# A hybrid decoder step on one core: the first token tile is normed by a diagonal matmul, and side work in the projection phase changes engine and place

## The chip, the core and the metric

The kernel runs on one core of a Trainium2 chip. The core has five engines with queues of their own: TensorE (PE, with the weight load shown apart as PEld), VectorE (DVE), ScalarE (ACT), GpSimd (POOL) and SyncE (SP), which here only starts DMA transfers. Each engine takes its instructions in the order in which the program lists them, so an instruction that waits holds up everything behind it on its engine. The metric is the device time of one execution in microseconds (us).

## The reference

The program is one inference step of one layer with three branches. Its beginning is what the change touches. The tokens x (1024 of a prompt, 64 of a sample) are normed, multiplied by a weight matrix, and the result is cut into the inputs of the branches:

```python
def rms_norm(x, g):
    xf = x.astype(jnp.float32)
    y = xf * lax.rsqrt(jnp.mean(xf * xf, axis=-1, keepdims=True) + EPS) * g.astype(jnp.float32)
    return y.astype(x.dtype)
...
    z = rms_norm(x, gain) @ w_in
    split_at = np.cumsum(IN_SIZES)[:-1].tolist()
    (rq, rk, rv, rg, pu, pg, nq, ck, cv, sk, sv, wk, wv, nbg, ng, mg) = jnp.split(z, split_at, axis=-1)
```

Retention takes rq, rk and rv, pooling takes pu, and sparse attention takes nq and the six key and value parts ck to wv. Gates merge the three, and one more matrix gives the output. All of this is in float32, and the kernel keeps that precision by holding each number as a float16 high half and a float16 low half (the remainder). A product is then three matmuls: high by high, low by high, high by low.

## The kernel before

The 1088 tokens are nine tiles of 128 (the ninth, number 8, is the sample and has 64). The function `phase_kv` is the first phase. It fills `self.xh` and `self.xl`, the normed tokens turned so that the 1024 channels lie on the partitions in 8 slices, and it projects each tile twice: `kv_tile` makes the keys, values and branch gates (792 columns, in PSUM tiles of 512 and 280), `q_tile` makes the queries (512 columns). The loop over `n` runs over the tiles in the order `TILES` = 0 to 6, 8, 7. At step n it norms the tile two places ahead, makes the keys and values of tile n, and makes the queries of tile n-1. Each PSUM tile of 512 columns is 24 matmuls (8 slices times 3).

`norm_tile` squares a tile on ACT with a sum over the channels (L352, L355), takes the power -1/2 on POOL (`rsqrt`, L381), and multiplies x by that factor and by the norm weights `gain` on DVE (L358). Tiles 0 to 2 are then turned by PE transposes (L370) into PSUM, and ACT and DVE copy the two halves out (L373, L374). Tiles 3 and later are split first, on ACT (L361) and POOL (L362), and turned by DMA transposes (L364).

`load_t` brings the weights in 8 slices by DMA and `wsplit` splits each into halves on ACT (L218) and DVE (L219). The buffers `raw` are two; four more slices use the memory of the query weights as `spare`. `input_sums` makes eight groups of sums of the normed tokens for a later phase (four additions on POOL, L1163; four subtractions on DVE, L1165; halves on ACT and DVE, L1166 and L1167; one DMA). `load_c` brings a block of 128 columns of weights for the phase after (`self.wng`). `cmp_prompt` needs the block means `cm` that PE makes of each tile's keys and values (L591).

The order of instructions on an engine is not the order of the code. A scheduler places each instruction as early as it thinks its inputs allow, so that work written late can stand early in a queue. Two means hold it back: `issue_after(ins)` puts instructions behind `ins` on its engine, and `behind()` does that for every instruction in the dictionary `self.marks`, one for each engine. Both only order a queue; they add no wait on the chip.

The rest of the program (attention of the prompt, retention, pooling, attention of the sample, output) follows `phase_kv`, and its code is the same in both kernels. Its first matmuls are those of `silu_c` (L298 to L300), which use the block of weights `self.wng`.

Of the kernel before, what the change touches and what calls it, by code (L numbers as in the profile page):

```python
# [20 lines left out]
P = 128  # L21
# [106 lines left out]
class Kern:  # L128
# [32 lines left out]
    def run(self):  # L161
# [3 lines left out]
        with ExitStack() as es:  # L165
# [7 lines left out]
            with ExitStack() as e1:  # L173
# [7 lines left out]
                deque(self.silu_c(sp, self.gc, C_NG, ps, self.wng), 0)  # L181
# [34 lines left out]
    def wsplit(self, hi, lo, raw):  # L216
        nc = self.nc
        nc.scalar.activation(hi, raw, AF.Copy, scale=WS)  # L218
        nc.vector.scalar_tensor_tensor(lo, raw, WS, hi, op0=ALU.mult, op1=ALU.subtract)  # L219
# [15 lines left out]
    def load_t(self, pool, cols, tag, bufs, out=None, spare=(), between=None):  # L235
# [5 lines left out]
        for k in range(8):  # L241
            if between and k == 4:
                between()
            if 3 <= k < 3 + len(spare):
                raw = spare[k - 3]
            else:
                raw = self.wtile([P, 1024], F32, "raw")
# [4 lines left out]
            self.wsplit(hi[:, k, :], lo[:, k, :], raw[:, :n])  # L252
# [15 lines left out]
    def proj_t(self, out, hi, lo, t, c0, n):  # L268
# [5 lines left out]
        for k in range(8):  # L274
# [4 lines left out]
            nc.tensor.matmul(out, xl, hi[:, k, c0:c0 + n], start=False, stop=(k == 7))  # L279
# [22 lines left out]
    def evac(self, out, c0, ps, n, m):  # L302

        nc = self.nc
        if m == P:
            nc.scalar.activation(out[:, c0:c0 + n], ps[:, :n], AF.Copy, scale=IWS)
            return
# [25 lines left out]
    def norm_tile(self, xp, ps, gain, t):  # L333
        nc, d = self.nc, self.d
        m = self.tm(t)
        x = xp.tile([P, 1024], F32, tag="x", name=self.nm("x"), bufs=2)
        src = d["x_sample"].rearrange("b t c -> (b t) c") if t == 8 else d["x_prompt"][0, t * P:(t + 1) * P, :]
        if t == 0:
            nc.sync.dma_start(x[:, :512], src[:, :512])
            nc.sync.dma_start(x[:, 512:], src[:, 512:])  # L340
            nc.sync.dma_start(gain, d["norm_gain"].broadcast_to([P, 1024]))
            nc.sync.dma_start(self.ident, d["c_ident"])
            nc.sync.dma_start(self.a4, d["c_a4"])
            nc.vector.tensor_copy(self.id16, self.ident)
        else:
            nc.sync.dma_start(x[:m], src)
        xs = xp.tile([P, 1024], F32, tag="xs", name=self.nm("xs"), bufs=2)
        ss = xp.tile([P, 2], F32, tag="ss", name=self.nm("ss"), bufs=2)
        cuts = (slice(0, 512), slice(512, 1024)) if t == 0 else (slice(0, 1024),)
        if t == 0:  # L350
            for i, c in enumerate(cuts):
                nc.scalar.activation(xs[:, c], x[:, c], AF.Square, accum_out=ss[:, i:i + 1])  # L352
            nc.vector.tensor_tensor(ss[:, 0:1], ss[:, 0:1], ss[:, 1:2], op=ALU.add)
        else:
            nc.scalar.activation(xs[:m], x[:m], AF.Square, accum_out=ss[:m, 0:1])  # L355
        self.rsqrt(ss[:m, 1:2], ss[:m, 0:1], 1.0 / 1024)
        for c in cuts:
            nc.vector.scalar_tensor_tensor(xs[:m, c], x[:m, c], ss[:m, 1:2], gain[:m, c], op0=ALU.mult, op1=ALU.mult)  # L358
# [54 lines left out]
    def bias_tables(self, bp, ps):  # L413
# [19 lines left out]
        nc.vector.tensor_copy(self.idb, self.ident)  # L433
# [1325 lines left out]
```

## Time and profile before

| what | value |
|---|---|
| runs | 1335.08, 1335.47 and 1340.86 us, median 1335.47 |
| the profiled execution | 1337.31 us, span from first to last instruction 1335.5 us |
| PE busy | 1263.3 us (95% of the span) |
| DVE, ACT, POOL busy | 860.3, 613.3 and 539.4 us (64%, 46%, 40%) |
| mean granted clock of TensorE | 0.989 of full speed |

An engine's busy time says how much of the span it had an instruction in work. PE is near its limit over the whole program, so that time can only be won where PE is idle or runs at its lower clock. The page's view in 40 slices shows PE's busy tenths 6, 7, 9, 9, 9 in the first five slices of 33.4 us each, and 9 in nearly all that follow.

### The profile page before, as it was taken

Reading aid. Unit: us, or ns where it says so; the run is one execution under the profiler, and the core shown is the slowest. Engines: PE = TensorE matmul, PEld = TensorE weight load, DVE = VectorE, ACT = ScalarE, POOL = GpSimd, SP = SyncE. Lnnn points to the kernel's source line nnn. Section 1 sums busy time; section 2 is a strip of 40 time slices with the busy share of each in tenths; the row PEclk is TensorE's granted clock in tenths of the full one; section 3 lists DMA queues with packets and bytes.
Section 4 is the critical chain, followed back from the end, with each engine's and each line's share of the span. In section 5 each row is a group of like instructions: output and inputs, shape, how many; then the busy total and the mean of one; then the engine's idle time right before and its main releaser. Section 6 shows DMA issues by size and latency. Waiting matters only on the chain. (4 is left out here: it accounts for less than half of the span.)

```text
span 1335.5 us, 27663 instructions
## 1 busy us (share of the span) xinstructions
PE 1263.3 (95%) x10572; PEld 852.2 (64%) x10572; DVE 860.3 (64%) x2164; ACT 613.3 (46%) x1434; POOL 539.4 (40%) x587
## 2 busy tenths in 40 slices
PE   6799999989999998999999999999999999998997
PEld 3345566667666665555555566667888888877444
DVE  6676225777776763767684757762388777789523
ACT  6533234666666763546554443433334333333112
POOL 2346112556666662245554461101134665455100
PEclk9899999999999999999999999999999999999999
DMA  8957412577998998342554154314232211343332
GB/s 269 207 124 166 76 48 68 110 126 141 148 181 173 172 185 184 95 124 70 160 134 96 47 147 110 80 41 166 55 104 68 60 48 49 97 128 94 129 99 80
DMA packets 311210, 155.63 MB, mean 117 GB/s; under 512 B 202849, under 2 KB 297025, under 8 KB 310660
## 3 DMA queue, kind: packets, MB, share of 16 engines
q1 hardware_dynamic: 280004, 122.88, 40.9%
q10 hardware_dynamic: 26336, 17.67, 4.7%
q0 software_dynamic: 4736, 13.31, 3.2%
q8 instruction: 83, 1.36, 0.5%
q14 instruction: 51, 0.42, 0.1%
HBM read 84.91 MB, written 23.55 MB: 81 GB/s over the span
## 5 line engine op out<-in xcount | busy, mean ns | idle before, releaser
L704 POOL TENSOR_TENSOR hl<-S,hl 128x640 f16<-128x640 f32 (+7 forms) x128 | 152.2, 1198 | 157.9 <-DVE hl L703 97.3
L298 PE MATMUL pj<-xh,whi 128*128 128x384 f16 (+1 forms) x480 | 153.5, 320 | 1.7 <-ACT qsts L643 1.7
L299 PE MATMUL pj<-xl,whi 128*128 128x384 f16 (+1 forms) x480 | 153.4, 320 | 0.0
L300 PE MATMUL pj<-xh,wlo 128*128 128x384 f16 (+1 forms) x480 | 153.4, 320 | 0.0
L277 PE MATMUL z<-rwh,xh 128*128 128x512 f16 x256 | 97.0, 379 | 0.0
L279 PE MATMUL z<-rwh,xl 128*128 128x512 f16 x256 | 97.0, 379 | 0.0
L278 PE MATMUL z<-rwl,xh 128*128 128x512 f16 x256 | 97.0, 379 | 0.0
L699 ACT ACTIVATE S<-S,nm 128x640 f32<-128x640 f32 (+7 forms) x128 | 93.7, 732 | 5.1 <-DVE hl L703 1.3
L300 PEld LDWEIGHTS <-wlo 128*128 128x128 f16 x672 | 66.0, 98 | 35.5 <-issue 1.7
L1434 POOL TENSOR_TENSOR ws<-raw 128x512 f32<-128x512 f32 x12 | 15.7, 1312 | 180.4 <-DMA raw<-w_in 154.2
L218 ACT ACTIVATE whi<-raw 128x1024 f16<-128x1024 f32 (+1 forms) x53 | 48.6, 917 | 86.8 <-PE pj L299 20.6
L299 PEld LDWEIGHTS <-whi 128*128 128x128 f16 x672 | 66.0, 98 | 34.6 <-issue 3.8
L298 PEld LDWEIGHTS <-whi 128*128 128x128 f16 x672 | 66.0, 98 | 33.6 <-issue 1.4
L1698 PE MATMUL py<-wo,mm 128*128 128x512 f16 (+2 forms) x408 | 83.5, 367 | 1.0 <-ACT mm L1651 1.0
L1487 DVE TENSOR_TENSOR q<-st,q 128x288 f32<-128x288 f32 (+1 forms) x168 | 71.1, 434 | 20.0 <-PE st L1478 18.6
L1270 PE MATMUL o<-vst,pt 128*128 128x64 f16 x528 | 57.9, 194 | 22.0 <-DMA pt<-hl 22.0
L279 PEld LDWEIGHTS <-xl 128*128 128x128 f16 x448 | 44.4, 99 | 48.3 <-issue 3.9
L277 PEld LDWEIGHTS <-xh 128*128 128x128 f16 x448 | 45.2, 101 | 45.4 <-issue 5.9
L278 PEld LDWEIGHTS <-xh 128*128 128x128 f16 x448 | 44.4, 99 | 42.4 <-issue 1.8
L795 DVE CUSTOM_DVE_ANT_0 S<-pn,tnear 128x256 f32<-128x256 f32 (+1 forms) x128 | 47.2, 403 | 32.3 <-PE pn L789 27.8
L1698 PEld LDWEIGHTS <-mm 128*128 128x128 f16 x408 | 39.4, 98 | 44.6 <-ACT mm L1651 1.5
L1270 PEld LDWEIGHTS <-pt 128*128 128x128 f16 x528 | 47.5, 98 | 31.5 <-DMA pt<-hl 28.2
(469 smaller groups left out, 4002.6 us busy)
## 6 DMA issues: line engine op xcount, KB each, us to landing
raw<-w_in SPq DMA_DIRECT2D x26, 512.0 KB
raw<-w_in ACTq DMA_DIRECT2D x18, 512.0 KB
x<-x_prompt SPq DMA_DIRECT2D x14, 512.0 KB
raw<-w_in SPq DMA_DIRECT2D x48, 128.0 KB
txd<-rso SPq DMA_DIRECT2D x8, 544.0 KB
q<-egd SPq DMA_DIRECT2D x16, 272.0 KB
s<-state_ret SPq DMA_DIRECT2D x16, 256.0 KB
o_ret_s<-s POOLq DMA_DIRECT2D x16, 256.0 KB
```

What stands on the lines that cost most here:

```text
L218: nc.scalar.activation(hi, raw, AF.Copy, scale=WS)
L277: nc.tensor.matmul(out, xh, hi[:, k, c0:c0 + n], start=(k == 0), stop=False)
L278: nc.tensor.matmul(out, xh, lo[:, k, c0:c0 + n], start=False, stop=False)
L279: nc.tensor.matmul(out, xl, hi[:, k, c0:c0 + n], start=False, stop=(k == 7))
L298: nc.tensor.matmul(out, hi[:, k, :], xh, start=(k == 0), stop=False)
L299: nc.tensor.matmul(out, hi[:, k, :], xl, start=False, stop=False)
L300: nc.tensor.matmul(out, lo[:, k, :], xh, start=False, stop=(k == 7))
L699: nc.scalar.activation(s[:, c0:c1], s[:, c0:c1], AF.Exp, bias=nm[:, br:br + 1], scale=0.125, accum_out=l[:, 0, br, r:r + 1])
L704: nc.gpsimd.tensor_tensor(hl[:, w:2 * w], s[:, d0:c1], hl[:, :w], op=ALU.subtract)
L1270: nc.tensor.matmul(out, lhs[0], rhs[0], start=start, stop=False)
L1487: nc.vector.tensor_tensor(out[:, c0:c0 + n], b, x[:, c0:c0 + n], op=ALU.add)
L1698: nc.tensor.matmul(py[:, :n], mm[:, k, t, a, e:e + P], b[:, k, cq], **fl)
```

## The change

The first tile gets a function of its own, `norm_first`. The squares of its second half are summed on DVE beside those of the first half on ACT. The power -1/2 of each token is put on the diagonal of a matrix `dg` (identity times a column), and x is turned and scaled at once by an fp32 matmul of x with `dg`. The norm weights then lie along the partitions (`gcol`, 8 columns), and the copies out of PSUM multiply by them, one copy for each of the 8 slices on ACT and on DVE. The weights come as two inputs that the host lays out: `gain_cols` (128x8) and `gain_rows` (128x1024, for the other tiles, loaded later). The identity is loaded third, and `c_a4` after the weights.

The slices of the key and value weights go to the spare memory from the second on (before: from the third). The second tile's norm, the later weight splits, the sums of `input_sums`, the load of `self.wng`, and two casts are tied behind marks; `input_sums` is spread over steps 4 to 8 as 1, 2, 2, 2, 1. POOL's subtraction of `norm_tile` (L362) and its additions of `input_sums` (L1163) go to DVE. The block means of a tile (`cmp_means`) are tied behind the last projection matmul, so that they follow the query projection, and `cmp_prompt` comes after the last `q_tile`. The sample's query tile gets a buffer of its own (`qs8`).

```diff
+                with self.behind():
+                    deque(self.silu_c(sp, self.gc, C_NG, ps, self.wng), 0)
...
         for k in range(8):
-            if between and k == 4:
-                between()
-            if 3 <= k < 3 + len(spare):
-                raw = spare[k - 3]
+            if between:
+                between(k)
+            if 2 <= k < 2 + len(spare):
+                raw = spare[k - 2]
...
+            if between and k:
+                self.marks = self.first[0 if k == 1 else 1]
+            with self.behind() if between and k else nullcontext():
+                split = self.wsplit(hi[:, k, :], lo[:, k, :], raw[:, :n])
+            if between:
+                self.marks = split
...
+    def norm_first(self, xp, ps):
+
+        nc, d = self.nc, self.d
+        x = self.load_x(xp, 0)
+        nc.sync.dma_start(self.ident, d["c_ident"])
+        gcol = xp.tile([P, 8], F32, name="gcol", bufs=1)
+        nc.sync.dma_start(gcol, d["gain_cols"])
...
+        nc.scalar.activation(xs[:, :512], x[:, :512], AF.Square, accum_out=ss[:, 0:1])
+        nc.vector.tensor_tensor_reduce(out=xs[:, 512:], in0=x[:, 512:], in1=x[:, 512:], scale=1.0, scalar=0.0,
+                                       op0=ALU.mult, op1=ALU.add, accum_out=ss[:, 1:2])
+        nc.vector.tensor_tensor(ss[:, 0:1], ss[:, 0:1], ss[:, 1:2], op=ALU.add)
+        self.rsqrt(ss[:, 1:2], ss[:, 0:1], 1.0 / 1024)
+        dg = xp.tile([P, P], F32, name="dg", bufs=1)
+        nc.vector.tensor_scalar(dg, self.ident, ss[:, 1:2], None, op0=ALU.mult)
+        self.first = []
+        for q in range(2):
+            tp = ps.tile([P, 4, P], F32, tag="tk", name=self.nm("tp"), bufs=2)
+            for k in range(4):
+                kk = q * 4 + k
+                nc.tensor.matmul(tp[:, k, :], x[:, kk * P:(kk + 1) * P], dg, start=True, stop=True)
+            for k in range(4):
+                kk = q * 4 + k
+                self.marks["ACT"] = nc.scalar.activation(self.xh[:, kk, :P], tp[:, k], AF.Copy, scale=gcol[:, kk:kk + 1])
+                self.marks["DVE"] = nc.vector.scalar_tensor_tensor(
+                    self.xl[:, kk, :P], tp[:, k], gcol[:, kk:kk + 1], self.xh[:, kk, :P],
+                    op0=ALU.mult, op1=ALU.subtract)
+            self.first.append(dict(self.marks))
...
-            nc.gpsimd.tensor_tensor(xd[:m, 1], xs[:m], xd[:m, 0], op=ALU.subtract)
+            nc.vector.tensor_tensor(xd[:m, 1], xs[:m], xd[:m, 0], op=ALU.subtract)
...
-                self.kv_tile(kp, bp, ps, kh, kl, cmt, TILES[n])
+                kvz = self.kv_tile(kp, bp, ps, kh, kl, TILES[n])
+            if n:
+                self.q_tile(kp, ps, qh, ql, TILES[n - 1])
             if n == NT:
                 self.cmp_prompt(kp, ps, cmt)
-            if n:
-                self.q_tile(kp, ps, qh, ql, TILES[n - 1])
+            if n < NT and TILES[n] < 8:
+                with self.tc.issue_after(self.marks["PE"].ins):
+                    self.cmp_means(ps, kvz, cmt, TILES[n])
...
-            if n >= 5:
-                next(sums, None)
-                next(sums, None)
+            with self.behind():
+                for _ in range((0, 0, 0, 0, 1, 2, 2, 2, 1, 0)[n]):
+                    next(sums)
             if n == 7:
-                self.wng = self.load_c(d["w_in"][0][:, C_NG:C_NG + P])
+                with self.behind():
+                    self.wng = self.load_c(d["w_in"][0][:, C_NG:C_NG + P])
...
-                    nc.gpsimd.tensor_tensor(f[:, i], self.xh[:, kk, c], self.xl[:, kk, c], op=ALU.add)
+                    nc.vector.tensor_tensor(f[:, i], self.xh[:, kk, c], self.xl[:, kk, c], op=ALU.add)
```

The order of instructions differs up to about row 1550 of PE's 20519, row 184 of DVE and row 137 of ACT, and is the same from there to the end. Three places show how.

The first is the start of DVE's queue. In these rows a row is a line of code, the operation, what it writes and what it reads; `ss` is the sum and the factor of a token, `kvl` the low half of a weight slice. Before:

```order
L353 TENSOR_TENSOR ss_123<-ss_123 128x1
L380 TENSOR_SCALAR ss_123<-ss_123 128x1
L344 CAST id_67<-ident 128x128
L358 SCALAR_TENSOR_TENSOR xs_122<-x_115,ss_123,gain 128x512 x2
L433 CAST idb<-ident 128x128
L219 SCALAR_TENSOR_TENSOR kvl_148<-raw_149,kvh_147 128x792
L374 TENSOR_TENSOR xl<-tp_131,xh 128x4x128
```

And now:

```order
L362 ISA xs_121,ss_122<-x_115 128x512
L362 ISA ss_122 128x1
L364 TENSOR_TENSOR ss_122<-ss_122 128x1
L413 TENSOR_SCALAR ss_122<-ss_122 128x1
L367 TENSOR_SCALAR dg<-ident,ss_122 128x128
L220 SCALAR_TENSOR_TENSOR kvl_159<-raw_160,kvh_158 128x792
L377 SCALAR_TENSOR_TENSOR xl<-tp_130,gcol,xh 128x128 x3
```

The scaling of 2 times 512 columns by `gain` and two casts of the identity have left the place ahead of PE's first work, and one multiplication of 128 columns stands there.

The second is ACT's queue where the queries of the first tile are copied out of PSUM (`qs<-pj`). `whi<-raw` splits weights of the next phase, `xd<-xs` is a tile's high half ahead of its DMA transposes. Before:

```order
L355 ACTIVATE xs_883,ss_884<-x_881 64x1024
L228 DMA raw_1648<-w_in 128x8x128
L218 ACTIVATE whi_1388<-raw_1386 128x1024
L361 CAST xd_772<-xs_766 128x1024
L619 ACTIVATE qs_470<-pj_445 128x8x64
L218 ACTIVATE whi_1650<-raw_1648 128x1024
```

And now:

```order
L394 CAST xd_621<-xs_615 128x1024
L314 ACTIVATE kvz_510<-pj_511 128x512
L389 ACTIVATE xs_911,ss_912<-x_909 64x1024
L602 CAST kd_565<-kvz_510 128x2x128
L621 CAST vst<-kvz_510 128x2x64
L670 ACTIVATE qs_479<-pj_454 128x8x64
L394 CAST xd_786<-xs_780 128x1024
```

The split of the next phase's weights has gone from ahead of the copy (it now stands some 50 rows further down), and so has one of the halves `xd`.

The third is PE's queue at the block means `cm` of one tile, beside the query projection `pj<-nqh` or `nql` of the tile before. Before:

```order
L278 LDWEIGHTS xh
L278 MATMUL pj_686<-nql,xh 128x512
L591 MATMUL cm_681<-a_68,kvz_612 128x4 x2
L279 LDWEIGHTS xl
L279 MATMUL pj_686<-nqh,xl 128x512
```

And now:

```order
L287 LDWEIGHTS xl
L287 MATMUL pj_695<-nqh,xl 128x512
L657 MATMUL cm_724<-a_68,kvz_626 128x4 x2
L458 MATMUL btp<-oh_734,rb 32x512
```

The means stood after 8 of the 24 matmuls of the query projection, and now stand after all of them.

## Rows read from the trace of the kernel before

**Rows 1.** Busy time by stretch: start:end, us, PE, PEld, DVE, ACT, POOL (instructions), PEclk, DMA, GB/s

```profile
8.94:37.07 28.13, 23.51 (x136) 14.08 (x137) 22.93 (x37) 22.16 (x40) 9.73 (x11) 1.00 0.87 277
37.07:68.43 31.36, 23.12 (x123) 12.15 (x121) 20.29 (x35) 15.24 (x28) 11.98 (x13) 0.89 0.89 196
68.43:161.21 92.78, 86.88 (x586) 48.25 (x585) 55.24 (x110) 31.03 (x74) 40.05 (x62) 0.98 0.58 126
```

**Rows 2.** PE's waits up to 175 us: line, waited for, total us, times, longest

```profile
PE tp L370 <- DVE xs L358: 10.7, 2, 8.9
PE tq L634 <- DVE qs L620: 5.9, 1, 5.9
PE cm L591 <- ACT kvz L306: 3.2, 2, 2.7
...
PE pj L278 <- DVE nql L219: 1.2, 1, 1.2
```

**Rows 3.** Timeline of the start: start, length, engine, line, operation [idle before, releaser]

```profile
4.46 0.63 ACT L352 ACTIVATE xs<-x 128x512 f32<-128x512 f32 x1
...
5.65 0.55 POOL L381 TENSOR_TENSOR ss<-ss,half 128x1 f32<-128x1 f32 x1 [5.21 <-DVE ss L380]
...
8.00 0.23 DVE L344 CAST id<-ident 128x128 f16<-128x128 f32 x1 [2.43 <-DMA ident<-c_ident]
8.14 1.41 DVE L358 SCALAR_TENSOR_TENSOR xs<-x,ss,gain 128x512 f32<-128x512 f32 x2
...
8.94 1.97 PE L370 MATMUL tp<-ident,xs 128*128 128x128 f32 x8 [8.94 <-DVE xs L358]
...
10.73 0.84 PE L277 MATMUL pj<-kvh,xh 128*128 128x512 f16 x2
```

**Rows 4.** Two stretches of the start, columns as in Rows 1

```profile
4.46:7.60 3.14, 0.00 (x0) 0.00 (x0) 0.31 (x2) 0.73 (x4) 0.55 (x1) 1.00 0.82 266
8.00:13.00 5.00, 4.06 (x15) 2.57 (x16) 4.77 (x9) 3.77 (x6) 0.00 (x0) 1.00 1.04 409
```

**Rows 5.** Timeline, an fp32 matmul that is no transpose (four in the program)

```profile
86.75 1.06 PE L425 MATMUL btp<-oh,rb 33*32 33x512 f32 x8
```

**Rows 6.** Timeline around the first query tile

```profile
54.71 1.06 ACT L218 ACTIVATE whi<-raw 128x1024 f16<-128x1024 f32 x1 [6.16 <-DMA raw<-w_in]
...
57.65 1.05 ACT L361 CAST xd<-xs 128x1024 f16<-128x1024 f32 x1 [1.88 <-DMA xl<-xd]
...
59.97 1.03 PE L634 MATMUL tq<-id,qs 128*128 128x128 f16 x8 [5.86 <-DVE qs L620]
```

**Rows 7.** Busy time of the stretch from 58.00, columns as in Rows 1

```profile
58.00:64.80 6.80, 4.83 (x21) 2.91 (x22) 4.71 (x8) 5.59 (x10) 3.77 (x4) 0.50 0.91 202
```

**Rows 8.** Timeline at the block means of the fifth step

```profile
79.41 1.10 ACT L1166 CAST rso<-rsf 128x1088 f16<-128x1088 f32 x1 [4.47 <-DVE rsf L1165]
...
81.06 0.61 PE L591 MATMUL cm<-a,kvz 128*128 128x4 f32 x4 [2.70 <-ACT kvz L306]
...
82.00 0.63 PE L278 MATMUL pj<-nql,xh 128*128 128x512 f16 x1
...
85.58 0.38 PE L278 MATMUL pj<-nql,xh 128*128 128x512 f16 x1
```

**Rows 9.** Groups by line and shape, 0 to 161 us: busy us, mean ns, idle before

```profile
L1163 POOL TENSOR_TENSOR rsf<-xh,xl 128x272 f32<-128x272 f16 x32 | 22.3, 727 | 16.5 <-DVE rso L1167 13.1 <-DMA xl<-xd 2.2 <-DVE xl L374 1.2
...
L1165 DVE TENSOR_TENSOR rsf<-rsf 128x272 f32<-128x272 f32 x32 | 22.5, 704 | 11.6 <-POOL rsf L1163 9.7
...
L1167 DVE TENSOR_TENSOR rso<-rsf,rso 128x1088 f16<-128x1088 f32 x8 | 10.5, 1311 | 7.6 <-ACT rso L1166 7.6
```

**Rows 10.** All instructions of line 1165: ns min/median/max, first and last start us

```profile
L1165 DVE TENSOR_TENSOR rsf<-rsf x32: 371/443/2247, 66.2 to 128.8; 128x272 f32<-128x272 f32 x32
```

**Rows 11.** Timeline of the phase's end

```profile
159.10 0.43 PE L641 MATMUL tq<-id,qs 64*64 64x64 f16 x8 [0.90 <-DVE qs L628]
...
161.21 0.48 PE L298 MATMUL pj<-xh,whi 128*128 128x384 f16 x1 [1.67 <-ACT qsts L643]
```

More of the change, by code (lines that the diff above doesn't have):

```diff
@@ L278, in proj_t @@
             nc.tensor.matmul(out, xh, lo[:, k, c0:c0 + n], start=False, stop=False)
-            nc.tensor.matmul(out, xl, hi[:, k, c0:c0 + n], start=False, stop=(k == 7))
+            self.marks["PE"] = nc.tensor.matmul(out, xl, hi[:, k, c0:c0 + n], start=False, stop=(k == 7))
     def cols2(self, out, xh, xl, hi, lo, c0, n):
@@ L305, in evac @@
         if m == P:
-            nc.scalar.activation(out[:, c0:c0 + n], ps[:, :n], AF.Copy, scale=IWS)
+            self.marks["ACT"] = nc.scalar.activation(out[:, c0:c0 + n], ps[:, :n], AF.Copy, scale=IWS)
             return
@@ L470, in phase_kv, with between @@
         gain = kp.tile([P, 1024], F32, name="gain", bufs=1)
-        self.norm_tile(kp, ps, gain, 0)
+        self.norm_first(kp, ps)
+        def between(k):
+            if k == 3:
+                x = self.load_x(kp, 1)
+                nc.sync.dma_start(gain, d["gain_rows"])
+                with self.behind():
+                    self.norm_tile(kp, ps, gain, 1, x)
         nq = [wk.tile([P, 8, 512], F16, name="nq" + x) for x in "hl"]
         spare = [x.rearrange("p k c -> p (k c)").bitcast(F32)[:, o:o + 1024] for x in nq for o in (0, 1024)]
-        kh, kl = self.load_t(wk, [(C_KV, 792)], "kv", 1, spare=spare, between=lambda: self.norm_tile(kp, ps, gain, 1))
+        kh, kl = self.load_t(wk, [(C_KV, 792)], "kv", 1, spare=spare, between=between)
         cmt = kp.tile([P, 2, 32], F32, name="cmt", bufs=1)
+        nc.sync.dma_start(self.a4, d["c_a4"])
+        with self.behind():
+            nc.vector.tensor_copy(self.id16, self.ident)
         for n in range(NT + 1):
@@ L557, in kv_tile @@
         if tk is None:
-            nc.sync.dma_start_transpose(self.kst[:, :, rows], kd.rearrange("p r g b a c -> p (r g b a c)"))
+            self.marks["SP"] = nc.sync.dma_start_transpose(self.kst[:, :, rows], kd.rearrange("p r g b a c -> p (r g b a c)"))
         elif t < 8:
@@ L587, in kv_tile @@
         if t < 8:
-            nc.vector.reciprocal(self.gate[:, t, :], ge)
-            cmps = ps.tile([P, 2, 4], F32, tag="cm", name=self.nm("cm"))
-            for a in range(2):
-                nc.tensor.matmul(cmps[:, a, :], kvz[:, a * P:(a + 1) * P], self.a4, start=True, stop=True)
-            for a in range(2):
-                nc.vector.tensor_scalar(cmt[:, a, 4 * t:4 * t + 4], cmps[:, a, :], self.pm[:, a:a + 1], None,
-                                        op0=ALU.add)
+            self.marks["DVE"] = nc.vector.reciprocal(self.gate[:, t, :], ge)
         else:
@@ L608, in kv_tile, with cmp_means @@
                                         ap=[[1, 8], [24, 8], [1, 1]]))
+        return kvz
+    def cmp_means(self, ps, kvz, cmt, t):
+        nc = self.nc
+        cmps = ps.tile([P, 2, 4], F32, tag="cm", name=self.nm("cm"))
+        for a in range(2):
+            nc.tensor.matmul(cmps[:, a, :], kvz[:, a * P:(a + 1) * P], self.a4, start=True, stop=True)
+        for a in range(2):
+            nc.vector.tensor_scalar(cmt[:, a, 4 * t:4 * t + 4], cmps[:, a, :], self.pm[:, a:a + 1], None, op0=ALU.add)
     def q_tile(self, kp, ps, qh, ql, t):
@@ L626, in q_tile @@
             nc.scalar.copy(qs[:64], qz[:, :, None, :].to_broadcast([64, 8, 2, 64]))
-            qt = kp.tile([P, 8, 2, 64], F16, tag="qs", name=self.nm("qs"))
+            qt = kp.tile([P, 8, 2, 64], F16, tag="qs8", name=self.nm("qs"), bufs=1)
             nc.vector.tensor_tensor(qt[:64, :, 0, :], qz, qs[:64, :, 0, :], op=ALU.subtract)
```

45 lines of the change are left out of this document (22 added, 23 removed).

## The prediction

> **What bounds the kernel now.** I read the busy shares first: PE is busy for 95% of the span, so only the places where it idles or runs slowly can pay. The view by stretch shows where these are. The change reorders the queues only up to the first matmul of `silu_c`, at 161.21 us, so I cut the time before it. PE does nothing for 8.94 us; then it is busy for 23.51 of 28.13 us, for 23.12 of 31.36 us at a mean clock of 0.89, and for 86.88 of 92.78 us at 0.98 [rows 1]. So the first 68 us hold most of what can be won.
>
> The list of PE's waits names the causes. The longest are the first transposes waiting for the scaled x, 8.9 us, then one wait of 5.9 us of the first query tile's transposes for `qs`, and 3.2 us in which the block means wait for a copy on ACT [rows 2]. The timelines then show what was late in each case.
>
> At the start, POOL has the factor of each token ready at 5.65 + 0.55 = 6.20 us. DVE, however, stands at the cast of the identity until its DMA lands at 8.00 (2.43 us idle), then scales 2 times 512 columns, and PE starts at 8.94 [rows 3]. The identity's transfer is queued behind the broadcast of the norm weights. In this time the DMA engines move 266 GB/s, against 409 GB/s a little later when the weight slices come [rows 4].
>
> At 59.97 PE has waited 5.86 us for `qs`. ACT's copy stood behind the split of `self.wng`, which had idled ACT for 6.16 us waiting for its weights, and behind a half `xd`, which had waited another 1.88 us for a DMA transpose to free its buffer [rows 6]. PE's clock then is 0.50 from 58.00 to 64.80 [rows 7].
>
> At 81.06 the block means wait 2.70 us for ACT, which had itself idled 4.47 us for the subtractions of `input_sums`; after that a 128x512 matmul takes 0.63 us instead of 0.38 [rows 8].
>
> **The change part by part.**
>
> *The start.* Removed from PE's path are the wait for the identity behind the norm weights and the scaling of 2 times 512 columns. The squares of the second half move to DVE. No row shows this reduction; the nearest is the scaling, 1.41 / 2 = 0.7 us for 512 columns, about the 0.63 us of ACT, so the sum of squares comes at most a few tenths earlier or later, and I take POOL's end at 6.2 as it is. Then one multiplication of 128 columns, for which the cast of the identity gives 0.23 us: PE starts at about 6.5 instead of 8.94. The identity now lies behind x alone, whose second half ACT read at 4.46, so I expect it by then or soon after.
>
> Against this, the eight transposes become eight plain fp32 matmuls. The fp32 matmul of `btp` shows what these cost: four in the program are eight instructions on PE, two passes each, and the four run side by side in 1.06 us, so one pass of 512 columns takes about 0.5 us at full clock and one of 128 about 0.13, or 0.26 at half clock [rows 5]. The transposes took 1.97 / 8 = 0.25 us each at the low clock [rows 3], so a pass costs what a transpose did, and there are 16. They take 3.9 us and end near 10.4; the first projection begins there instead of at 10.73. The Trainium skill ("TensorE: Matmul & The Clock Gate", section "Terms") calls the transpose mode four times faster for FP32. By that the eight matmuls would take 8 x 4 x 0.25 = 7.9 us; by the rows it is two times, and I go by the rows. The eight small copies on ACT and on DVE, at 0.23 us or so each (the cast again), lie beside these passes except the last.
>
> What PE then waits for is the stream of weight slices. The 3.14 us up to 7.60 carried 266 GB/s; at 409 GB/s the same bytes take 2.04, so the stream is 1.1 us earlier if the laid-out norm weights move like the rest. Two small transfers fewer stand ahead of the slices, some 0.5 us of issue. I take **-1.6** for this stretch. The bounds are 0 and -4.6: the first if the waits inside move, since the small matmul `pmps` now stands in PE's queue before the third slice is done and needs two transfers (`c_a4`, `pe_cmp`) that lie behind six weight slices; the second is all the idle time there, 28.13 - 23.51.
>
> *37 to 68 us.* The split of `self.wng` and one `xd` no longer stand ahead of the copy of `qs`, and the 512 KB load of that block no longer competes with the DMA transposes. Gone are 5.9 us of waiting and half of the 4.83 us that PE was busy at the low clock, 2.4 us: **-8.3**. Something comes back. In DVE's new order the low halves of the second tile's keys, for which PE waits early in the first query tile, stand behind POOL's old subtraction (1024 columns, 1.3 us by the row of 1088 columns [rows 9]), two copies of a third tile (0.7 each, by the scaling) and the scaling of the fifth tile (1.4): 4.1 us of work. PE has some other matmuls by then; I take 3.3 us of waiting, where the old order had 31.36 - 23.12 - 5.86 = 2.4 of other idle time, so +1.0. A wait of this length was followed by about 3.4 us of half clock in the old trace, which cost 1.7 [rows 8]; I add that: **+2.7** in all, between 0 and +6.8 (all 4.1 waited for, 1.7, and 1.0 more for the last query weights, whose loads now follow DMA transposes in SP's queue).
>
> *68 to 161 us.* The means go behind the query projection, by when their input is long copied, and POOL no longer delays `input_sums`: the 3.2 us of waits go, and with them the low clock of this stretch, (1 - 0.98) x 92.78 = 1.9: **-5.1**. DVE takes 32 additions of 272 columns, 0.727 us each on POOL, and POOL's six subtractions. On DVE I take 0.443, the median of the subtractions of the same size [rows 10]: 14.2 us, and 6 x 1.3 = 7.8. But the 32 subtractions had taken 22.5 us in total, up to 2.25 each, while POOL was adding; at the median they take 14.2, which gives 8.3 back. DVE's 55.24 us become at most 55.2 + 14.2 + 7.8 - 8.3 = 68.9 of some 87.7, 79%, so this is hidden. It costs when a wait of ACT or PE falls in behind a block of eight such operations, 3.5 us; the key halves and query copies have at least the 5 us of the next projection for it.
>
> *The end.* The wait of 0.90 for the buffer of the sample's queries goes with `qs8`. The wait of 1.67 for the copy `qsts` [rows 11] stays in another shape: the second pair of `cmp_prompt` matmuls now stands directly ahead of `silu_c`, and needs the small copies of the first pair, which ACT and DVE interleave with the query copies and the last `input_sums`. I reckon **+0.4**, between -2.6 (both waits gone) and +2.
>
> The sum is -1.6 - 8.3 + 2.7 - 5.1 + 0.4 = **-11.9 us**. From there on both programs have the same order and wait for the same things, so I carry it to the end. Against the profiled execution's 1337.3 us that is 1325.4; the median of the runs lies 1.8 us below that execution, so I forecast 1323.6.
>
> **The rivals.** *The waits move.* The start gives nothing because PE stands at `pmps`, and 37 to 68 us give back 6.8 instead of 2.7: -8.3 + 6.8 - 5.1 + 0.4 = -6.2, about 1329.3; a little more waiting for the query weights makes it 1332. For it speaks that ACT, DVE and SP wait in turn for each other in this stretch; against it, that the old wait had two long transfers behind it that are now elsewhere.
>
> *Plain fp32 matmuls cost four transposes each.* The first projection starts 4 us later than I reckoned and everything behind it too: 1327.6. The skill's rule above gives this; the `btp` row speaks against it.
>
> *DVE becomes the bound.* If an addition on DVE takes as long as the subtractions did at worst, DVE's work exceeds the 87.7 us that PE needs in tiles 3 to 8. That begins at 0.443 + (87.7 - 68.9) / 32 = 1.03 us each; at 1.8 it is 25 us too much, 13 more than is won, and the time is 1348. The subtractions at 2.25 us speak for it; that POOL does nothing long beside DVE any more speaks against it.
>
> *No net change.* The marks only order queues. If the scheduler's old order was waiting for the same transfers that any order must wait for, the phase ends where it did: 1335. The 6.16 us of ACT waiting for weights that nobody needed yet speaks against it.
>
> **How the numbers follow.** My forecast has a chance of 0.60, the moving waits 0.20, the dear fp32 matmuls 0.05, no change 0.07, DVE as the bound 0.08. About 0.5% (6.7 us, so below 1328.8) is what a measurement of this kernel can tell from no change. Faster by more than that are the forecast, the fp32 case and a third of the moving waits: 0.72. Within it lie the rest of the moving waits and no change, 0.20, and a weak form of the DVE case, 0.01; slower is the rest, 0.07. The range goes from 1317 (start at its bound of -4.6, nothing given back in 37 to 68 us, nothing lost at the end: -18.0 or 1317.5) up to 1333, which takes in the moving waits; outside it are most of the no-change case and DVE as the bound.
>
> **What would show it.** PE's first matmul at 6.5 us with 16 fp32 instructions at 0.25 us; the first query projection some 2 us before 37.07; no wait of PE over 3 us between 30 and 70 us, and the key projection of tile 3 begun by 60 instead of 68.43; no wait for the means; DVE's additions at 0.4 to 0.5 us; the first `silu_c` matmul at about 149 us; the same length from there to the end. I would be wrong if ACT again stood behind a transfer in front of `qs`, if PE lost its clock in the new waits more than once, or if the later phases gave the time back.

## The result and the profile after

The changed kernel takes 1323.44 us (median; 1322.17 to 1326.12) against 1338.16 us for the kernel before in the same comparison: a ratio of 0.9892, 95% interval 0.9855 to 0.9928. A second comparison on another chip gave 1323.26 us and 0.9906 (0.9882 to 0.9930). The profiled execution took 1326.12 us, with a span of 1324.4.

I cut the new trace at the same five events as the old one: the first matmul, the first query projection, the key projection of the fourth tile, the last query projection, and the first matmul of `silu_c`. Columns as in [rows 1]; first the kernel after, then the stretches of before that were not shown yet.

```profile
6.48:37.38 30.90, 27.40 (x145) 17.83 (x146) 22.56 (x45) 20.81 (x41) 3.90 (x5) 0.89 0.84 258
...
37.38:60.62 23.24, 20.81 (x123) 11.17 (x121) 14.73 (x29) 12.50 (x26) 5.64 (x8) 1.00 0.77 172
60.62:137.36 76.74, 76.74 (x536) 44.34 (x536) 49.58 (x121) 29.09 (x65) 17.81 (x33) 1.00 0.65 135
137.36:149.33 11.97, 8.14 (x50) 4.55 (x50) 10.74 (x30) 6.38 (x14) 0.00 (x0) 0.83 0.68 170
...
149.33:1324.40 1175.07, 1130.61 (x9733) 777.72 (x9732) 763.17 (x1977) 545.06 (x1291) 477.97 (x498) 0.99 0.47 111
```

```profile
68.43:151.92 83.49, 80.15 (x542) 44.93 (x540) 52.35 (x100) 26.65 (x61) 40.05 (x62) 0.98 0.61 133
151.92:161.21 9.29, 6.73 (x46) 3.33 (x46) 2.88 (x10) 4.38 (x14) 0.00 (x0) 0.96 0.34 58
161.21:1335.50 1174.29, 1129.77 (x9732) 777.68 (x9731) 759.66 (x1974) 542.27 (x1288) 476.88 (x498) 0.99 0.47 109
```

Event by event: the first query projection starts at 37.38 instead of 37.07 (+0.31); from there to the fourth key projection 23.24 instead of 31.36 [rows 1] (-8.12); to the last query projection 76.74 instead of 83.49 (-6.75), with PE busy all the time; to `silu_c` 11.97 instead of 9.29 (+2.68). The sum is -11.88, and what follows is 0.78 longer. The start gained nothing, and the end lost; the middle won more than either. The two traces thus differ by 11.1 us, the medians by 14.7 here and by 13.3 in the second comparison; the runs of the kernel before alone spread from 1335.08 to 1341.84 us in the first.

PE's waits up to 165 us, columns as in [rows 2], without the 6.5 us for its first matmul. The waits of 5.9 for `qs` and 3.2 for the means are gone; the longest between 30 and 70 us is the 1.0 for `kvz`.

```profile
PE tq L692 <- DVE qs L679: 2.0, 1, 2.0
PE vc L562 <- DVE kcst L560: 1.5, 1, 1.5
PE pj L285 <- ACT kvh L219: 1.4, 1, 1.4
PE pj L285 <- ACT kvz L314: 1.0, 1, 1.0
...
PE tk L609 <- DVE xl L407: 0.7, 1, 0.7
PE tk L609 <- ACT kd L602: 0.6, 1, 0.6
```

The timeline of the start, columns as in [rows 3], and a stretch of it, columns as in [rows 1], show why 2.5 us less before the first matmul came to nothing.

```profile
6.48 3.79 PE L373 MATMUL tp<-dg,x 128*128 128x128 f32 x16 [6.48 <-DVE dg L367]
...
8.59 0.37 ACT L376 ACTIVATE xh<-tp,gcol 128x128 f16<-128x128 f32 x1 [0.29 <-PE tp L373]
9.23 0.34 DVE L377 SCALAR_TENSOR_TENSOR xl<-tp,gcol,xh 128x128 f16<-128x128 f32 x1
...
9.61 0.37 ACT L376 ACTIVATE xh<-tp,gcol 128x128 f16<-128x128 f32 x1 [0.65 <-DVE xl L377]
...
10.01 0.35 DVE L377 SCALAR_TENSOR_TENSOR xl<-tp,gcol,xh 128x128 f16<-128x128 f32 x1 [0.43 <-ACT xh L376]
...
14.67 0.85 ACT L219 ACTIVATE kvh<-nqh 128x792 f16<-128x792 f32 x1
14.81 0.35 DVE L377 SCALAR_TENSOR_TENSOR xl<-tp,gcol,xh 128x128 f16<-128x128 f32 x1 [0.44 <-ACT xh L376]
...
15.58 0.81 PE L285 MATMUL pj<-kvh,xh 128*128 128x512 f16 x2 [1.37 <-ACT kvh L219]
...
17.17 0.77 PE L487 MATMUL pmps<-a,pe 32*128 32x1 f32 x3 [0.78 <-DMA pe<-pe_cmp]
```

```profile
15.60:22.40 6.80, 6.02 (x22) 3.91 (x22) 5.31 (x8) 5.93 (x10) 0.56 (x1) 0.50 0.65 191
```

The sixteen fp32 instructions take 3.79 us, as reckoned. But the copies take turns: the high copy of 9.61 starts when the low copy of the slice before ends (9.23 + 0.34), and the low copy of 10.01 when that high copy has ended (9.61 + 0.37). Eight pairs run from 8.59 to 15.16 us. Weight splits on ACT and DVE stand among and behind them (the low copy of 9.23 stood behind one on DVE), PE idles 1.37 us for one on ACT (14.67), and 0.78 more in `pmps`.

The larger loss follows: from 15.6 to 22.4 us the granted clock is 0.50 (1.2 GHz), where the kernel before had 1.00 [rows 1]. PE is busy for 6.02 us of it; half of that, an estimated 3.0 us, is what the clock costs. PE's idle time up to the first query projection is even less than before, 30.90 - 27.40 = 3.5 against 4.6 us; its busy time is 3.9 us more.

The Trainium skill ("PSUM — Partial Sum Buffer", section "PSUM bank collisions raise a hardware error") says that two engines must not be in one PSUM bank and partition group together, and that the compiler's scheduler puts a dependency between such accesses. The timeline agrees: the copies of the start form two sequences, as for two PSUM tiles, and within neither do two overlap.

The end, DVE and PE:

```profile
142.36 1.50 DVE L1214 TENSOR_TENSOR rsf<-xh,xl 128x272 f32<-128x272 f16 x4
...
143.77 1.22 DVE L220 SCALAR_TENSOR_TENSOR wlo<-raw,whi 128x1024 f16<-128x1024 f32 x1
144.91 0.43 DVE L1216 TENSOR_TENSOR rsf<-rsf 128x272 f32<-128x272 f32 x1
145.26 0.68 DVE L679 TENSOR_TENSOR qs<-qz,qs 64x512 f16<-64x512 f32 x1
...
145.99 0.63 PE L692 MATMUL tq<-id,qs 64*64 64x64 f16 x8 [1.98 <-DVE qs L679]
...
148.71 0.69 PE L562 MATMUL vc<-wcvd,cmr 64*128 64x64 f32 x2 [1.53 <-DVE kcst L560]
```

The last group of `input_sums` and a weight split stand in DVE's queue ahead of the sample's queries, which PE waits 1.98 us for.

### The profile page after: what moved, and what is told of

Its sections match the earlier page's. It is cut to its first block, busy times and chain, and to the rows that moved or that the text cites. A ratio compares the mean times of both kernels' runs of the same rounds, so it can differ in the third digit from the quotient of the medians.

```text
span 1324.4 us, 27672 instructions
## 1 busy us (share of the span) xinstructions
PE 1263.7 (95%) x10580; PEld 855.6 (65%) x10580; DVE 863.0 (65%) x2209; ACT 615.9 (47%) x1438; POOL 506.1 (38%) x549
```

## The experiments

My theory after the result: the gain is the wait of ACT's queue for `self.wng`, the means in the middle of a projection, and POOL's slow work; the start is eaten by the copies' turns; the end is lost to the late sums. The rivals are in the expectations. One table holds the events of all traces (start in us of the first query projection, the fourth key projection, the last query projection and `silu_c`; the rest of the span behind that; then the median of the runs, and its ratio to the kernel before in the same comparison, with the 95% interval).

| kernel | query 1 | key 4 | last query | silu_c | rest | median | ratio |
|---|---|---|---|---|---|---|---|
| before | 37.07 | 68.43 | 151.92 | 161.21 | 1174.3 | 1338.16 | 1 |
| changed | 37.38 | 60.62 | 137.36 | 149.33 | 1175.1 | 1323.44 | 0.9892 (0.9855 to 0.9928) |
| e_again (changed) | 36.80 | 58.88 | 135.62 | 147.58 | 1173.8 | 1323.26 | 0.9906 (0.9882 to 0.9930) |
| e_wng | 37.52 | 62.42 | 142.16 | 155.56 | 1175.9 | 1331.92 | 0.9964 (0.9935 to 0.9993) |
| e_pool | 37.87 | 60.66 | 141.40 | 151.76 | 1176.2 | 1329.57 | 0.9946 (0.9923 to 0.9970) |
| e_cmmid | 36.23 | 57.57 | 138.75 | 151.10 | 1172.6 | 1325.80 | 0.9922 (0.9895 to 0.9948) |
| e_oldstart | 36.25 | 55.90 | 133.45 | 145.47 | 1176.7 | 1325.84 | 0.9912 (0.9885 to 0.9938) |
| e_oldstart2 (the same) | 38.77 | 58.44 | 135.99 | 148.26 | 1176.0 | 1322.03 | 0.9895 (0.9871 to 0.9920) |
| e_copies | 35.51 | 55.96 | 134.15 | 146.09 | 1177.8 | 1323.27 | 0.9886 (0.9835 to 0.9937) |
| e_sums | 36.77 | 59.19 | 135.94 | 146.33 | 1172.9 | 1323.23 | 0.9899 (0.9868 to 0.9929) |
| e_all | 35.11 | 54.77 | 132.32 | 142.74 | 1172.9 | 1322.50 | 0.9897 (0.9871 to 0.9923) |
| e_all2 (the same) | 32.32 | 52.91 | 133.92 | 144.40 | 1180.2 | 1323.05 | 0.9902 (0.9872 to 0.9933) |
| e_oldall | 38.79 | 58.44 | 135.99 | 146.97 | 1179.8 | 1326.30 | 0.9915 (0.9887 to 0.9943) |
| e_best | 35.33 | 54.99 | 133.58 | 143.60 | 1178.3 | 1320.49 | 0.9879 (0.9850 to 0.9908) |

The same code differs from trace to trace by up to 2.8 us in an event of the front and by 7.3 us in the rest (e_all, e_all2), so single traces tell only larger things apart.

**The load let loose (e_wng).**

```diff
-                with self.behind():
-                    deque(self.silu_c(sp, self.gc, C_NG, ps, self.wng), 0)
+                deque(self.silu_c(sp, self.gc, C_NG, ps, self.wng), 0)
...
             if n == 7:
-                with self.behind():
+                if True:
                     self.wng = self.load_c(d["w_in"][0][:, C_NG:C_NG + P])
```

> Only the load of the output gates' weights and its split are let loose again (not tied behind marks), all else as changed. Theory: the 8.1 us gained between the first query projection and the fourth key projection are the wait of ScalarE's queue for this load; so that stretch goes back from 23.2 us to 29 to 32 us, ScalarE shows a wait of 4 us or more before the split, and the time is 1329 to 1332 us. Rival: the gain comes from the other edits of this stretch (the low halves on VectorE, the order of the copies); then the stretch stays at 23 to 25.5 us, the split waits under 2 us, and the time is 1323 to 1326 us.

ACT's timeline has the wait back, in two pieces:

```profile
54.75 1.06 ACT L218 ACTIVATE whi<-raw 128x1024 f16<-128x1024 f32 x1 [2.70 <-DMA raw<-w_in]
...
60.53 1.06 ACT L218 ACTIVATE whi<-raw 128x1024 f16<-128x1024 f32 x1 [3.19 <-DMA raw<-w_in]
...
61.50 0.58 ACT L669 ACTIVATE qs<-pj 128x512 f16<-128x512 f32 x1
61.97 0.40 ACT L313 ACTIVATE kvz<-pj 128x280 f32<-128x280 f32 x1
```

Behind the second split stand the copies of `qs` and `kvz`; PE waits 3.6 us for the latter, up to 62.42, and from 60.6 us on its granted clock is 0.50:

```profile
37.52:62.42 24.90, 20.36 (x115) 10.71 (x113) 15.75 (x29) 13.60 (x27) 5.55 (x8) 0.96 0.92 206
60.60:67.40 6.80, 4.91 (x18) 2.08 (x18) 4.71 (x9) 4.96 (x10) 0.55 (x1) 0.50 0.85 199
62.42:142.16 79.74, 79.67 (x545) 45.56 (x545) 53.32 (x131) 30.22 (x67) 17.59 (x33) 0.97 0.65 138
142.16:155.56 13.40, 7.66 (x50) 4.18 (x50) 7.60 (x21) 5.06 (x13) 0.00 (x0) 0.89 0.61 140
```

The mechanism and the median (8.5 us over the changed kernel) are the theory's. The size in its stretch is not: 24.90 instead of 29 to 32, which lies in the rival's range of 23 to 25.5. Beside 1.8 us for the wait (62.42 - 60.62), the next stretch is 3.0 longer (79.74 - 76.74; by its mean clock of 0.97 about 2.4 of that is the low clock) and the end loses 1.4. So this edit accounts for some 4.8 of the 8.1 us that the change won up to the fourth key projection. The other 3.3 are left to the remaining reordering there (the half `xd` ahead of `qs` in [rows 6], for one). No run undid that alone, so it is not shown.

**The work back on GpSimd (e_pool).**

```diff
-            nc.vector.tensor_tensor(xd[:m, 1], xs[:m], xd[:m, 0], op=ALU.subtract)
+            nc.gpsimd.tensor_tensor(xd[:m, 1], xs[:m], xd[:m, 0], op=ALU.subtract)
...
-                    nc.vector.tensor_tensor(f[:, i], self.xh[:, kk, c], self.xl[:, kk, c], op=ALU.add)
+                    nc.gpsimd.tensor_tensor(f[:, i], self.xh[:, kk, c], self.xl[:, kk, c], op=ALU.add)
```

> Only the two groups of element-wise work that went from GpSimd to VectorE (low halves of the normed tiles, sums of the gate inputs) are put back on GpSimd, all else as changed; the compressed means stay behind the query projection. Theory: most of the 6 us gained between 60 and 137 us are GpSimd's slow operations and what they held up; so that stretch takes 80 to 83 us instead of 76.7 us and the time is 1327 to 1331 us. Rival: the gain is the compressed means' new place alone; then the stretch is 76.5 to 78.5 us and the time 1322 to 1326 us.

80.74 us and 1329.57: the numbers of the theory. But the loss is not spread over the stretch:

```profile
60.66:120.30 59.64, 59.64 (x410) 34.36 (x409) 29.60 (x63) 20.10 (x42) 24.65 (x38) 1.00 0.67 141
60.66:141.40 80.74, 78.49 (x538) 44.82 (x538) 42.48 (x88) 27.55 (x61) 37.45 (x59) 0.98 0.61 133
```

For 59.64 us PE never waits, with POOL busy for 24.65 of them. All 4.0 us come from one wait of 2.2 us at 124.27 for `kd` (the low half of the sample's keys), and the half clock from 125.7 on. The timeline shows what was ahead of `kd`:

```profile
120.54 1.60 DVE L220 SCALAR_TENSOR_TENSOR wlo<-raw,whi 128x1024 f16<-128x1024 f32 x1 [0.72 <-ACT whi L219]
122.06 1.95 DVE L1216 TENSOR_TENSOR rsf<-rsf 128x272 f32<-128x272 f32 x3
123.93 0.28 DVE L603 TENSOR_TENSOR kd<-kvz,kd 64x128 f16<-64x128 f32 x1
...
124.27 0.23 PE L614 MATMUL tk<-id,kd 64*128 64x64 f16 x2 [2.25 <-DVE kd L603]
```

The same two instructions in the trace of the changed kernel:

```profile
123.60 0.28 DVE L603 TENSOR_TENSOR kd<-kvz,kd 64x128 f16<-64x128 f32 x1
...
124.72 0.23 PE L614 MATMUL tk<-id,kd 64*128 64x64 f16 x2
```

A split and three subtractions stood ahead of `kd`; while POOL added, the split took 1.60 us instead of 1.23 and the first subtraction 0.93 instead of 0.44. Yet `kd` is only 0.33 us later than in the changed kernel, where a split and four additions stand ahead of it. What differs is PE's queue: the query projection begins at 120.3 us in both traces, and the transposes `tk` that read `kd` stand after 7 of its 24 matmuls here and after 20 there. At the earlier place the changed kernel would have waited some 2 us too. The kernel before has `tk` after 7 matmuls as well (135.59 us), but no wait there, because its `kd` (133.76) came before the query projection (133.97). So the 4.0 us come from where `tk` stands once the work has changed engine. They are no wait of the kernel before that the change took away, and they don't show that POOL's slowness cost anything.

**The means in the middle (e_cmmid).**

```diff
+            if mid and k == 3:
+                with self.tc.issue_after(self.marks["PE"].ins):
+                    means = mid()
+            with self.tc.issue_after(means.ins) if mid and k >= 3 else nullcontext():
+                nc.tensor.matmul(out, xh, hi[:, k, c0:c0 + n], start=(k == 0), stop=False)
```

> Only the matmuls of the block means are put back into the middle of the query projection (after three of its eight slices), where the kernel before had them; all else as changed. Theory: their place is what cost the kernel before its waits between 68 and 152 us; then TensorE waits for ScalarE's copy of kvz at these matmuls for 2 to 4 us in sum, a half clock of 3.4 us or more follows, and the stretch from the fourth key projection to the last query projection takes 79 to 82 us instead of 76.7 us, the time 1326 to 1329 us. Rival: with the two groups of work off GpSimd ScalarE's copies come early enough anywhere; then the stretch stays at 76.5 to 77.5 us and the time at 1322 to 1325 us.

```profile
68.58 1.04 ACT L398 CAST xd<-xs 128x1024 f16<-128x1024 f32 x1 [3.96 <-DMA xl<-xd]
...
69.53 0.59 ACT L318 ACTIVATE kvz<-pj 128x512 f32<-128x512 f32 x1
...
70.17 0.73 PE L662 MATMUL cm<-a,kvz 128*128 128x4 f32 x4 [2.04 <-ACT kvz L318]
```

```profile
57.57:138.75 81.18, 78.88 (x537) 44.51 (x536) 49.23 (x121) 30.23 (x67) 18.47 (x33) 0.98 0.63 128
70.50:73.90 3.40, 3.40 (x11) 1.42 (x11) 2.27 (x10) 1.29 (x6) 1.02 (x2) 0.50 1.06 187
```

81.18 instead of 76.74, through a wait of 2.04 us and 3.4 us of half clock: the theory. ACT was late for another reason than in [rows 8], though: its copy stood behind a half `xd` that had waited 3.96 us for a DMA transpose, not behind the sums. The median is 2.5 us over that of e_again on the same chip, with overlapping intervals; the trace settles it, not the time.

**The old start (e_oldstart, e_oldstart2).** `norm_first` is given the transposes, the scaling on DVE and the two copies of 128x512 of before.

> The start of before (transposes by the identity, gain on VectorE, two copies of 128x512) in the otherwise changed kernel. Theory: the diagonal gained nothing, because the eight pairs of small copies take turns on one PSUM tile and end at 15.16 us; so the first query projection starts at 37.0 to 38.0 us (37.38 with the diagonal, 37.07 before) and the time is 1322 to 1326 us. Rival: the new start is worth the forecast 1.6 us, and something else of the change (the later loads behind marks) lost as much before 37 us; then the first query projection comes at 39.0 us here and the time is about 1325.5 us.

> The old start in the otherwise changed kernel once more, to see how much a start varies from one execution to the next: its first projection of queries came at 36.25 us, with the two other edits at 38.79 us. Theory: the start varies by 1 to 2.5 us with the landing of x and the norm weights, so that one trace of each doesn't tell the two starts apart; the first query projection starts between 36 and 39 us, not at 36.25 us within 0.3, and the median time stays 1 to 4 us over the changed kernel's (1324.3 to 1327.5 us). Rival: the old start is truly 1 us shorter, the first query projection starts at 36.0 to 36.5 us and the fourth key projection before 56.5 us again.

36.25, then 38.77 with the same code: the first expectation missed on both sides, the second held in that a start varies, but its median, 1322.03, lies below the 1324.3 to 1327.5 expected. PE's first matmul came at 8.32 and 8.96 (9.34 in e_oldall), because DVE waits 2.2 to 2.5 us for the norm weights; with the diagonal it came at 6.33 to 6.65 in all traces. Over all kernels with the diagonal and its copies in turns the first query projection comes at 36.2 to 37.9, with the old start at 36.3 to 38.8: these traces tell no gain from either.

**The copies set apart (e_copies).**

```diff
             for k in range(4):
                 kk = q * 4 + k
                 self.marks["ACT"] = nc.scalar.activation(self.xh[:, kk, :P], tp[:, k], AF.Copy, scale=gcol[:, kk:kk + 1])
+            for k in range(4):
+                kk = q * 4 + k
                 self.marks["DVE"] = nc.vector.scalar_tensor_tensor(
```

> In the new start the four high copies of a PSUM tile are written ahead of its four low copies, so that the two engines do not take turns slice by slice. Theory: the copies' turns set the start; 12 steps of about 0.36 us from 8.6 us on end at 13.0 to 13.5 us instead of 15.16 us, TensorE's wait of 1.37 us in the first projection goes, the first query projection starts at 34 to 36.2 us instead of 37.38 us (the lower end if the half clock of 15.6 to 22.4 us goes too), and the time is 1319.5 to 1322.5 us. Rival: the weight slices' transfers and splits set the first projection; then the first query projection stays at 37.0 to 37.7 us and the time at 1322 to 1326 us.

```profile
8.72 1.14 ACT L376 ACTIVATE xh<-tp,gcol 128x128 f16<-128x128 f32 x4 [0.61 <-PE tp L373]
...
9.89 1.13 DVE L379 SCALAR_TENSOR_TENSOR xl<-tp,gcol,xh 128x128 f16<-128x128 f32 x4 [0.77 <-ACT xh L376]
...
10.49 1.16 ACT L376 ACTIVATE xh<-tp,gcol 128x128 f16<-128x128 f32 x4
...
11.83 1.12 DVE L379 SCALAR_TENSOR_TENSOR xl<-tp,gcol,xh 128x128 f16<-128x128 f32 x4
```

Now ACT's second group (10.49) runs beside DVE's first, on the other PSUM tile, and the copies end at 12.95 instead of 15.16. The wait of 1.37 us is gone. In all four traces with this edit the first query projection comes at 32.3 to 35.5 us and the fourth key projection at 52.9 to 56.0. The half clock that began between 15.6 and 17.7 us in all six traces with copies in turns is in none of these four, nor in those of the old start. It comes later there instead: in three of the four, and in all three traces of the old start, it begins between 30.9 and 32.2 us, around the end of a wait of 2.4 to 3.8 us for ACT's copy `kvz`. In e_copies that is a wait for the means:

```profile
30.53 0.53 PE L659 MATMUL cm<-a,kvz 128*128 128x4 f32 x3 [2.39 <-ACT kvz L314]
```

In e_all2, where this wait is 1.4 us, no half clock follows it, and the first query projection comes 2.8 to 3.2 us before that of the other three. The rest of the expectation failed: the median, 1323.27, is that of the changed kernel.

**The sums one step earlier (e_sums).**

```diff
-                for _ in range((0, 0, 0, 0, 1, 2, 2, 2, 1, 0)[n]):
+                for _ in range((0, 0, 0, 0, 2, 2, 2, 2, 0, 0)[n]):
```

> The sums of the gate inputs are dealt out 2, 2, 2, 2, 0 over the last five steps instead of 1, 2, 2, 2, 1, so that none is left for VectorE beside the sample's queries and the last block keys. Theory: the sums in VectorE's queue make the 1.98 us wait for the low half of the sample's queries and most of the 1.53 us wait for the block keys; without them the stretch from the last query projection to silu_c takes 8.5 to 10 us instead of 11.97 us and the time is 1320 to 1323 us. Rival: these waits are the chain between ScalarE and VectorE itself, and the stretch stays over 11.3 us; or the sums only move and the fifth step waits for them by as much (fourth key projection to last query projection 78 us or more), and the time stays at 1322 to 1326 us.

```profile
PE vc L562 <- DVE kcst L560: 1.9, 1, 1.9
PE tq L692 <- DVE qs L679: 0.5, 1, 0.5
```

The end takes 10.39 us: between the two expectations. The wait for the sample's queries shrinks from 2.0 to 0.5 as the theory said; that for the block keys stays, so the sums did not make it. The median is the changed kernel's.

**Three edits (e_all, e_all2)**: those of e_copies and e_sums, and `cmp_weights` behind the first key projection.

> The changed kernel itself once more, as the measure for the others on this chip. Every theory: 1321 to 1326 us, the fourth key projection at 60.6 us and the first silu_c matmul at 149.3 us. If the half clock of 15.6 to 22.4 us comes from the order of the work it is there again; if it is chance, it is gone and the fourth key projection starts 2 to 3 us earlier.

> Three edits together: the four high copies ahead of the four low ones in the start, the weights of the block means after the first key projection in TensorE's queue, and the sums dealt out 2, 2, 2, 2, 0. Theory: the gains of the front add up: 3.2 us by the end of the fourth key projection, 0.4 us for the transfer that the small matmul waits for, 2 to 3 us at the end of the front; the first silu_c matmul starts at 142.5 to 144.5 us instead of 149.3 us, and the time is 1316 to 1320 us. Rival: what the front gains is lost later, in further stretches of half clock (the run with the split copies was 3.2 us ahead at 139 us and 0.5 us at the end); then silu_c starts at 142.5 to 144.5 us all the same, but the rest takes 1177 to 1180 us instead of 1175 us and the time is 1320 to 1324 us.

> The kernel with the three edits once more, with more runs, because its profiled execution took 1317.44 us and its other runs 1321 to 1324 us. Theory: the front is won in every execution (first silu_c matmul at 142.5 to 145 us again) and the runs differ in what comes behind; the median over the runs is 1317 to 1321 us. Rival: the early front is paid back behind it; the median is 1321.5 to 1324 us, with the profiled execution's rest over 1175 us.

In e_again the half clock was there again (from 16.6 us), and the fourth key projection came 1.7 us earlier all the same. In e_all and e_all2 `silu_c` came at 142.74 and 144.40, 3 to 7 us before the two traces of the changed kernel, yet the medians fell by less than 1 us: the events are the theory's, the times (1316 to 1320 and 1317 to 1321 expected) the rival's, although the rest of e_all is short. Its trace is of the fastest of its four runs, 1317.44 us. The two traces of this one program show how wide the rest is: over 315 us in the middle (retention) one is busy on PE for 311.18 us, the other for 304.04.

```profile
525.00:840.00 315.00, 311.18 (x2190) 184.69 (x2189) 214.83 (x626) 156.12 (x447) 134.13 (x199) 0.99 0.41 105
```

```profile
525.00:840.00 315.00, 304.04 (x2098) 179.14 (x2099) 211.23 (x614) 155.09 (x445) 134.81 (x199) 0.98 0.41 104
```

There the second waits longer for ACT (`ah`, 5.8 against 2.9 us, three waits in each) and for transfers. Whether an early front causes that is open: the rest was 1172.9 to 1180.2 us in the four traces with the copies apart, 1172.6 to 1176.2 in the six with them in turns.

**The block values on other PSUM tiles (e_best), the old start with the two other edits (e_oldall).**

```diff
-            vc = ps.tile([P, 64], F32, tag="kc", name=self.nm("vc"), bufs=2)
+            vc = ps.tile([P, 512], F32, tag="pj", name=self.nm("vc"), bufs=3)[:, :64]
```

> The three edits, and the two products of the block values get PSUM tiles of the projections' tag instead of sharing two tiles with the block keys. Theory: the wait of 1.86 us for the block keys' low half is the wait for their PSUM tile; it goes, the stretch from the last query projection to silu_c takes 8.2 to 9.2 us instead of 10.42 us, and the time is 1 to 2 us below that of the kernel with three edits. Rival: the small copies on ScalarE and VectorE are the chain, and the stretch stays over 10 us.

> The start of before (transposes by the identity, two copies of 128x512), with the two other edits (weights of the block means after the first key projection, sums dealt out 2, 2, 2, 2, 0). Theory: the old start and the new one with its copies set apart are worth the same within 1 us; the fourth key projection starts at 54 to 56 us and the first silu_c matmul at 142 to 144.5 us, the time within 2 us of the kernel with three edits. Rival: the diagonal is worth the forecast 1.6 us once its copies don't take turns; then both come at least 1.5 us later here than with the three edits (54.77 and 142.74 us).

In e_best the wait for `kcst` is gone, and `silu_c` waits 1.7 us for the copy `qsts` instead; the end takes 10.02 against 10.42, as the rival had it: the sample's queries are the longer chain. The time, 1320.49, is the lowest median here, but its interval overlaps the changed kernel's. In e_oldall the rival held: both events come at least 2.5 us after those of e_all and e_all2, so by these traces the diagonal gains once its copies don't take turns; the first trace of the old start (fourth key projection at 55.90) lies at the edge of the others (52.9 to 56.0), so how much is open. Its time, 1326.30, is 3 to 6 us over the kernels with the copies apart, with overlapping intervals.

## Why the prediction was right

The time, the event at `silu_c` (about 149; 149.33) and the equal length behind it came as forecast. Three of the five terms did not, and a fourth was small. That their errors (+1.9 at the start, -2.5 from 37 to 68 us, -1.7 up to the last query projection, +2.3 at the end) cancel is luck, and so is how close the median came: the second trace of the same kernel has `silu_c` at 147.58.

- *The start, -1.6.* Failed: +0.31. The step that failed is that the eight small copies on each engine "lie beside these passes except the last". The price of 0.23 us was that of an SBUF cast; out of PSUM they took 0.37 and 0.35, and they took turns. Besides, the 3.0 us that the half clock from 15.6 us on cost stood in no term. The passes (16 in 3.79 us, 3.9 forecast) and PE's start (6.48) were right. The price of a pass "at the low clock" fits the durations (128x512 matmuls took 0.63 us at 10.05 and 0.38 at 13.38 in the changed kernel, the two lengths of [rows 8]), but the granted clock reads 1.00 there, before [rows 4] and after. By the rule of the Trainium skill weighed there ("TensorE: Matmul & The Clock Gate", section "Terms") they would have taken 7.9 us; the trace disagrees. With the copies apart the gain against 37.07 was 1.6 us in e_copies.
- *37 to 68 us, -8.3.* The mechanism is shown by e_wng, with 4.8 us of it. *What comes back, +2.7*: mis-sized. The 3.3 us of waiting reckoned for the second tile's key halves were two waits of 0.7 and 0.6, no half clock followed, and next to nothing came back (8.12 of the 8.3).
- *68 to 161 us, -5.1.* Right in kind, small: -6.75 up to the last query projection. e_cmmid and e_pool, each undone alone, gave back 4.4 and 4.0 us, together more than the 6.75. The one bears out the waits for the means; the other does not bear out "POOL no longer delays `input_sums`", since its 4.0 us are a wait that the kernel before did not have. No run undid both together, so what the move off POOL is worth is not shown. DVE's additions took the 0.44 us forecast (32 of them at a median of 434 ns, the subtractions at most 443), and DVE was busy for 60.3 of 88.7 us from the fourth key projection to `silu_c`, so it became no bound.
- *The end, +0.4.* Mis-sized: +2.68. The wait behind the small copies of the first pair (1.53) was named there, but the wait for the sample's queries, of which the forecast had said that its 0.90 goes with `qs8`, became 1.98, because of what stood ahead in DVE's queue; e_sums took 1.6 of the 2.7 back.

Of the rivals, the moving waits were half true: the start gave nothing, though `pmps` cost only 0.78 of it, and 37 to 68 us gave nothing back. One sign of being wrong came true by the letter, PE losing its clock in new waits more than once (at 15.6 and at 145.3 us); the time held all the same.

## What to carry to other kernels

Before counting small copies as hidden, look which memory they share: two engines that copy from one PSUM tile in turns are a chain of single latencies, and grouping all copies of one engine before those of the other lets the next tile run beside. Here that showed in the events of the start, not in the median. Work that nobody needs yet costs most when its wait heads a queue; tie it behind the work that is needed, then look again at the last place where it can still be dealt out, since the end of a phase has no cover. A total that comes out right says little of its terms: cut both traces at the same events before you believe a step. And when undoing an edit costs what you expected, look whether the instruction that waits still stands at the same place of its queue.

## What the runs showed of the hardware

In the changed kernel two waits of PE, 0.5 us up to 13.38 and 1.4 us up to 15.58, were followed by 6.8 us at a granted clock of 0.50 (1.2 GHz) from 15.6 us on. While GpSimd added beside it, a split on VectorE took 1.60 us instead of 1.23, and the addition 1.67 instead of 0.69 (e_pool, 120.5 to 122.7 us). Two executions of one program differed by 7.3 us in its last 1180 us with the same instructions, nearly as much as the dearest single edit here changed the median (8.5 us, e_wng). A reduction on VectorE (512 columns, squares and sum) took 0.69 us and 0.08 to read the sum, as long as the scaling of the same size.
